# The mixer of a two-layer encoder on one Trainium2 core: background jobs on a credit clock, or one written order

## The chip, the cores and the metric

The kernel runs on one core of a Trainium2 chip. Its engines are PE (TensorE, matmuls and transposes), DVE (VectorE), ACT (ScalarE), POOL (GpSimd) and SP (SyncE, which here only issues DMAs). Each engine runs its own instructions strictly in program order, so an instruction that waits holds back everything behind it on that engine. The metric is the device time of one execution in microseconds (us), as the median of runs. Beside it stands the span of the profiled execution, from its first to its last instruction, to which all times of rows refer.

## What is computed

One sequence of 512 rows and 1024 columns goes through two layers. Only the first half of the first layer, the conv and state-space mixer, is touched by the change:

```python
def conv_ssm_layer(h, w_in, ...):              # h = rms_norm(x, mix_norm)
    z = h @ w_in                               # 1024 -> 512 (za) + 512 (zg) + 512 (u)
    ya = conformer_conv(za, zg, ...)           # za*sigmoid(zg), 31 taps, layer norm, silu
    yb = s5_mixer(u, ...)                      # scan forwards and backwards, 64 complex states a group
    return concatenate([ya, yb]) @ w_out
def s5_direction(u, ...):                      # once on u, once on u flipped in time
    bu = einsum('bsgc,gnc->bsgn', u, b)        # 32 groups of 16 channels
    s = associative_scan(a, coef * bu)
    return einsum('bsgn,gcn->bsgc', s, c)
```

After it come a gated feed-forward layer, a neighbourhood attention and a second feed-forward layer, whose code is the same before and after.

## The kernel before

The input projection `z` is three groups of fp32 matmuls: 4 weight chunks of 512 KB for `u`, 4 for the gate `zg` and 4 for `za`. A chunk is used by 8 products of 128x512 outputs (the trace counts each fp32 product as two matmul rows). The `u` group is issued at once. The 64 products of `zg` and `za` are handed out one by one by `heavy(n)`, which issues the next n of them on PE, so that PE has work between the small steps of the state-space part.

The state-space part cuts the sequence into 64 chunks of 8 rows and the 32 groups into 8 pieces of 4 groups. For every piece i there are:

- `make_pb(i)`: DVE builds the B products (six operations of 128x512) in a buffer;
- `piece_t(i)`: PE transposes them (P), ACT copies the two results (`ppb`) and fills `CB`;
- the K matmuls, whose result ACT copies to `kf`;
- the v matmuls (`U` is the transposed `u`), whose result ACT copies to `vt`;
- `g_turn(i)`: DVE multiplies phase tables, ACT copies one third of them with its sign changed;
- `g_scan(i)`: ACT fills the decays `dk` (tile rstdB), DVE turns v by the phases, runs two scans, turns the result back and writes the states S.

In the code of before, these DVE jobs are Python generators in a list (`bgV`). `tick(ns)` gives the list credit in nominal nanoseconds, and the jobs' DVE instructions are issued as the credit lasts; `finish(job)` issues the rest of a job where its result is needed. The loop issues `piece_t(i)`, then `heavy(2)`, then for the piece before it K, `heavy(1)`, v, and at the end `heavy(3)`. The backward half of v is turned round by a second ACT copy with a negative step. The B products have three buffers of their own.

The weights come through `Weights`. The first 12 chunks are used as they are, through all nine weight buffers (tags wraw, whi, wlo, three each). All later chunks are split into a high part (ACT, `whi`) and a low part (DVE, `wlo`), up to two chunks ahead of their use.

Behind the pieces, `to_chunks(an, ...)` transposes the gated input of the convolution (64 small PE transposes, 8 ACT copies). 112 ACT operations then build the banded tap matrices, PE convolves in 16 steps, and DVE evacuates 4 times and takes row sums. In the same stretch DVE builds Q (48 operations), the output matrices of the scan, again on credit: `tick(1350)` at each convolution step. `out_y` uses Q on PE; `ln_mean` and `ln_scale` are the layer norm; then the two branches are transposed (cT, yT), and `out_half` starts the output projection (`wo`).

Of the kernel before, what the change touches and what calls it, by code (L numbers as in the profile page):

```python
# [9 lines left out]
F32 = mybir.dt.float32  # L10
# [3 lines left out]
ALU = mybir.AluOpType  # L14
# [7 lines left out]
HP = (2, 1, 3)  # L22
XT = 600
UT = 5200
MT = 6000
H1 = 4
# [4 lines left out]
ZT, ME, ZC = 500, -4000, -1000  # L31
# [25 lines left out]
class Weights:  # L57
# [4 lines left out]
    def __init__(self, nc, pool, aps, whole=0):  # L62

        self.nc, self.pool, self.aps, self.whole = nc, pool, aps, whole
        self.raw, self.hl = {}, {}
        self.n_raw = self.n_hl = self.pos = 0
        self.on_pool, self.charge = (), None

    def load(self):
        i = self.n_raw  # L70
        if i >= len(self.aps):
            return
        ap = self.aps[i]
        a, b = ap.shape[1], ap.shape[2]
        tag = "wraw"
        if i < self.whole:
            tag = ("wraw", "whi", "wlo")[i % 3]
        t = self.pool.tile([P, a, b], F32, tag=tag, name=tag, bufs=self.RAW)
        self.nc.sync.dma_start(out=t, in_=ap)
        self.raw[i] = t  # L80
        self.n_raw += 1
# [40 lines left out]
def tile_hybrid_encoder(ctx, tc, x, mix_norm, ffn_norm, ffn_w_gate, ffn_w_up, ffn_w_down,  # L122
# [219 lines left out]
    def big4(shape):  # L342
        return ep.tile(shape, F32, tag="big4", name="big4", bufs=3)
# [22 lines left out]
    A.activation(out=un[:, 0, 0], in_=ones[:, 0:16], func=AF.Silu)  # L366
# [29 lines left out]
    W.load()  # L396
# [7 lines left out]
    W.load()  # L404
# [106 lines left out]
    def g_params():  # L511
# [61 lines left out]
        make_pb(0)  # L573
        job_phase.append(bgV.add(g_phase()))
        make_pb(1)
        make_pb(2)

# [9 lines left out]
    NPC, job_phase = 8, []  # L587
    PB, PBS, job_pb = {}, [P, 4, 8, 16], []
# [7 lines left out]
    def make_pb(i):  # L596
        PB[i] = big4([P, 2, 4, 8, 16])
        job_pb.append(bgV.add(g_pb(i)))
# [16 lines left out]
    job_par = bgV.add(g_params())  # L615
    tick(3000)
    xT, pxs = [], []
    xg = xp.tile([P, KD, S], F32, tag="xgh", name="xg")
    for k in range(KD):
        ps = (psa if k < 4 else psb)("xT")  # L620
        for j in range(4):
            PE.transpose(out=ps[:, j * P:(j + 1) * P], in_=xn[j][:, k * P:(k + 1) * P], identity=ident)
        pxs.append(ps)
        if k == 0:
            ps = psb("vec0")
            PE.transpose(out=ps[:, 0:16], in_=vecs[0:16], identity=ident[0:16, 0:16])
            V.tensor_copy(out=col[:, 0:16], in_=ps[:, 0:16])
        t = xtile("xT")
        A.activation(out=t, in_=pxs[k], func=AF.Copy)
        A.activation(out=xg[:, k], in_=pxs[k], func=AF.Copy, scale=col[:, R_MIX0 + k:R_MIX0 + k + 1])  # L630
        xT.append(t)
        tick(XT)
    W.ahead()
# [3 lines left out]
    for i in range(4):  # L637
# [16 lines left out]
        tick(UT)  # L654
        if i == 1:
            ps = psb("vec")
# [16 lines left out]
            V.tensor_tensor(out=gqk, in0=col[:, R_QK:R_QK + 1], in1=col[:, R_QK + 1:R_QK + 2], op=ALU.mult)  # L673
        if i == 2:
            for r in range(2):
                ps = psb("ct")
                for t in range(4):
                    PE.transpose(out=ps[:, t * P:(t + 1) * P],
                                 in_=cnat[r][:, t].rearrange("p d n -> p (d n)"), identity=ident)
                A.activation(out=CT[:, r], in_=ps.rearrange("p (g c) -> p g c", c=16), func=AF.Copy,  # L680
                             scale=-1.0 if r else 1.0)
    for j in range(4):
        A.activation(out=un[:, :, j], in_=pu[j].rearrange("p (g c) -> p g c", c=16),
                     func=AF.Copy, scale=rs0[:, j:j + 1])
# [40 lines left out]
    heavy(H1)  # L725
# [16 lines left out]
    to_chunks(un, U)  # L742

# [7 lines left out]
    vin, phase, job_scan = {}, {}, []  # L751
# [43 lines left out]
    ppb = ep.tile([P, 2, 2, 4, P], F32, tag="un", name="ppb")  # L795

    def piece_t(i):
        bgV.finish(job_pb[i])
        for q in range(2):
# [4 lines left out]
            A.activation(out=ppb[:, i % 2, q], in_=ps.rearrange("p (g n) -> p g n", g=4), func=AF.Copy)  # L804
# [5 lines left out]
    def piece_m(i):  # L810
        g0 = 4 * i
        pb, cb, pp = PB.pop(i), CB[i % 2], ppb[:, i % 2]
        def part_k():
            pk = psb("K")
            for g in range(4):
                for q in range(2):
                    w = pb[:, q, g].rearrange("p b c -> p (b c)")
                    for c in range(0, P, KW):
                        PE.matmul(out=pk[c:c + KW, g * 32:g * 32 + 32], lhsT=w[:, c:c + KW],
                                  rhs=cb[:, q, g].rearrange("p d c -> p (d c)"),  # L820
                                  start=(q == 0), stop=(q == 1))
            A.activation(out=kf[:, :, g0:g0 + 4],
                         in_=pk[:, 0:128].rearrange("p (g d c) -> p d g c", g=4, d=2), func=AF.Copy)

        part_k()
        heavy(HP[1])
# [11 lines left out]
        job_scan.append(bgV.add(g_scan(i)))  # L838

    bgV.finish(job_par)  # L840
    bgV.finish(job_phase[0])
    for v, q, r, sg in ((0, 0, 0, 1.0), (0, 1, 1, 1.0), (1, 0, 1, -1.0), (1, 1, 0, 1.0)):
        A.activation(out=low[v][:, :, :, q], in_=et[:, r, :, 0].rearrange("p e g -> p g e"), func=AF.Copy,
                 scale=sg)
    for i in range(NPC + 1):
        if i < NPC:
            piece_t(i)
            heavy(HP[0])
        if i > 0:
            if i > 2:  # L850
                bgV.finish(job_scan[i - 3])
            bgV.add(g_turn(i - 1))
            piece_m(i - 1)
            if i + 2 < NPC:
                make_pb(i + 2)
            if i == NPC:
                for h in range(2):
                    PL.tensor_tensor(out=pair[:, 64 * h:64 * h + 64], in0=ident[:, 0:64], in1=ident[:, 64:128], op=ALU.add)
                PL.tensor_scalar(out=pair, in0=pair, scalar1=1.0 / 512, scalar2=1.0, op0=ALU.mult, op1=ALU.mult)
                dm = pbp([P, G, 16])  # L860
                PL.tensor_tensor(out=dm, in0=dcol.unsqueeze(2).to_broadcast([P, G, 16]),
                                 in1=dmask.unsqueeze(1).to_broadcast([P, G, 16]), op=ALU.mult)
            tick(MT if i < NPC else ME)
            heavy(HP[2])
# [19 lines left out]

    heavy(100)
    V.tensor_reduce(out=mask16, in_=ident.rearrange("p (b c) -> p c b", c=16), axis=AX.X, op=ALU.add)
    for j in job_scan:
        bgV.finish(j)
# [60 lines left out]
    for b in range(4):  # L949
        ps = psa("conv")  # L950
        for gi in range(4):
# [10 lines left out]
            tick(1350)  # L962
# [551 lines left out]
```

## Time and profile before

| | |
|---|---|
| median of 3 runs | 1292.23 us (1291.77 to 1293.13) |
| the profiled execution | 1291.65 us |
| its span | 1289.7 us |
| PE busy | 1225.2 us, 95% of the span |
| DVE busy | 675.1 us, 52% |
| ACT busy | 471.4 us, 37% |
| POOL busy | 38.1 us, 3% |

The busy shares are averages over stages with different limits. The mixer takes the first 305 us or so; in it the engines take turns in ending the waits, while later PE is busy almost without a break. In the rows, "idle before" is the time the engine stood still ahead of an instruction, with what ended it.

### The profile page before, as it was taken

The numbers are of one execution on the slowest core, as the hardware profiler recorded it, in microseconds if no ns is written. First come the engines' busy times: TensorE is split into PE (matmuls) and PEld (weight loads), VectorE is DVE, ScalarE is ACT, GpSimd is POOL, SyncE is SP. The second block draws the span as 40 slices with busy tenths as digits, with TensorE's granted clock in tenths as the row PEclk, the third lists the DMA queues.
The fourth block names the chain that finished last, engine by engine and source line by source line (L and its number), as shares of the span: only waits on it lengthen the run. The fifth ranks groups of instructions, "written<-read, shape, count | busy, mean of one in ns | idle before, by whom it ended". The sixth has DMA issues, their size and how long they took to land.

```text
span 1289.7 us, 16189 instructions
## 1 busy us (share of the span) xinstructions
PE 1225.2 (95%) x6427; PEld 966.2 (75%) x6427; DVE 675.1 (52%) x1166; ACT 471.4 (37%) x830; POOL 38.1 (3%) x90
## 2 busy tenths in 40 slices
PE   4988867899999999999999999999999999999998
PEld 2544457788888888888888888667888888888886
DVE  4778875866444444433335563664544444443321
ACT  4335277554322333222233544653332223332110
POOL 1000000000000000000000000430000000000000
PEclk9998889899999999999999999999999999999999
DMA  8600140033333333333344542222333333332241
GB/s 158 179 2 1 49 104 2 17 99 100 97 98 99 98 97 94 95 91 95 101 141 127 153 142 72 83 75 71 93 99 98 98 98 98 98 98 82 95 134 33
DMA packets 173155, 118.04 MB, mean 92 GB/s; under 512 B 21193, under 2 KB 153593, under 8 KB 173080
## 3 DMA queue, kind: packets, MB, share of 16 engines
q1 hardware_dynamic: 172616, 115.92, 31.5%
q10 hardware_dynamic: 400, 1.07, 0.4%
q8 instruction: 50, 0.82, 0.3%
q14 instruction: 25, 0.20, 0.1%
q0 software_dynamic: 64, 0.03, 0.0%
HBM read 109.04 MB, written 7.96 MB: 91 GB/s over the span
## 4 chain that ended last, share of the span: by engine, by line
PE 82%; ACT 3%; DVE 1%; issue 0%; POOL 0%; ACTq 0%; DVEq 0%; POOLq 0%
PE gate L208 6%; PE up L208 6%; PE gate L207 6%; PE up L207 6%; PE up L206 6%; PE gate L206 6%; PE qkv L1379 3%; PE qkv L1381 3%; PE qkv L1380 3%; PE dn L208 3%; PE dn L207 3%; PE dn L206 3%; PE dn L1480 3%; PE dn L1478 3%; PE dn L1479 3%; PE o L1341 2%
## 5 line engine op out<-in xcount | busy, mean ns | idle before, releaser
L98 DVE TENSOR_TENSOR wlo<-wraw,whi 128x1024 fp32r<-128x1024 f32 x176 | 212.9, 1213 | 256.8 <-ACT whi L96 255.5
L96 ACT ACTIVATE whi<-wraw 128x1024 fp32r<-128x1024 f32 x176 | 183.4, 1044 | 283.5 <-issue 113.9
L206 PE MATMUL gate<-xgh,whi 128*128 128x512 f32 x352 | 137.2, 390 | 0.0
L206 PE MATMUL up<-xgh,whi 128*128 128x512 f32 x352 | 137.1, 390 | 0.0
L208 PE MATMUL gate<-xgh,wlo 128*128 128x512 f32 x352 | 137.0, 389 | 0.0
L208 PE MATMUL up<-xgh,wlo 128*128 128x512 f32 x352 | 137.0, 389 | 0.0
L207 PE MATMUL gate<-xgl,whi 128*128 128x512 f32 x352 | 136.9, 389 | 0.0
L207 PE MATMUL up<-xgl,whi 128*128 128x512 f32 x352 | 136.9, 389 | 0.0
L1163 DVE TENSOR_TENSOR fu<-up,rstdB 128x512 f32<-128x512 f32 x44 | 30.4, 691 | 113.4 <-PE up L208 113.4
L1165 ACT ACTIVATE gh<-fu 128x512 fp32r<-128x512 f32 x44 | 27.8, 632 | 150.8 <-DVE fu L1164 150.8
L207 PEld LDWEIGHTS gate<-xgl,whi 128*128 128x128 f32 x352 | 66.1, 188 | 13.9
L206 PEld LDWEIGHTS up<-xgh,whi 128*128 128x128 f32 x352 | 66.2, 188 | 13.8
L207 PEld LDWEIGHTS up<-xgl,whi 128*128 128x128 f32 x352 | 66.0, 188 | 13.7
L206 PEld LDWEIGHTS gate<-xgh,whi 128*128 128x128 f32 x352 | 66.0, 187 | 13.7
L208 PEld LDWEIGHTS gate<-xgh,wlo 128*128 128x128 f32 x352 | 66.1, 188 | 13.5
L208 PEld LDWEIGHTS up<-xgh,wlo 128*128 128x128 f32 x352 | 66.0, 188 | 13.6
L206 PE MATMUL dn<-gh,whi 128*128 128x512 f32 x176 | 69.3, 394 | 0.0
L207 PE MATMUL dn<-gl,whi 128*128 128x512 f32 x176 | 69.3, 394 | 0.0
L208 PE MATMUL dn<-gh,wlo 128*128 128x512 f32 x176 | 69.3, 394 | 0.0
L1480 PE MATMUL dn<-whi,gl 128*128 128x512 f32 x176 | 69.2, 393 | 0.0
L1478 PE MATMUL dn<-whi,gh 128*128 128x512 f32 x176 | 69.0, 392 | 0.0
L1379 PE MATMUL qkv<-whi,xgh 128*128 128x512 f32 x176 | 68.8, 391 | 0.0
(306 smaller groups left out, 2077.2 us busy)
## 6 DMA issues: line engine op xcount, KB each, us to landing
wraw<-in_ffn_w_gate_dram SPq DMA_DIRECT2D x44, 512.0 KB
wraw<-in_ffn_w_up_dram SPq DMA_DIRECT2D x44, 512.0 KB
wraw<-in_ffn_w_down_dram SPq DMA_DIRECT2D x38, 512.0 KB
wraw<-in_na_w_qkv_dram SPq DMA_DIRECT2D x24, 512.0 KB
bt<-bd SPq DMA_DIRECT2D x8, 640.0 KB
wraw<-in_ab_w_out_dram SPq DMA_DIRECT2D x8, 512.0 KB
wraw<-in_na_w_out_dram SPq DMA_DIRECT2D x8, 512.0 KB
wraw<-in_ffn_w_down_dram SPq DMA_DIRECT2D x8, 384.0 KB
```

The lines of the kernel that those rows point to most:

```text
L96: self.nc.scalar.activation(out=hi, in_=raw, func=AF.Copy)
L98: eng.tensor_tensor(out=lo, in0=raw, in1=hi.bitcast(F32), op=ALU.subtract)
L206: PE.matmul(out=o, lhsT=lh, rhs=rh, start=start, stop=False)
L207: PE.matmul(out=o, lhsT=lh, rhs=rl, start=False, stop=False)
L208: PE.matmul(out=o, lhsT=ll, rhs=rh, start=False, stop=stop)
L1163: V.tensor_tensor(out=u, in0=pu, in1=rB, op=ALU.mult)
L1379: PE.matmul(out=pq[j], lhsT=lh, rhs=wh[:, kk], start=(k == 0), stop=False)
L1380: PE.matmul(out=pq[j], lhsT=lh, rhs=wl[:, kk], start=False, stop=False)
L1381: PE.matmul(out=pq[j], lhsT=ll, rhs=wh[:, kk], start=False, stop=(k == 7))
L1478: PE.matmul(out=pd[j], lhsT=gh[:, k, c], rhs=wh[:, kk], start=(k == 0), stop=False)
L1479: PE.matmul(out=pd[j], lhsT=gh[:, k, c], rhs=wl[:, kk], start=False, stop=False)
L1480: PE.matmul(out=pd[j], lhsT=gl[:, k, c], rhs=wh[:, kk], start=False, stop=(k == NF - 1))
```

## The change

The mixer's background jobs are taken out of the credit list and written in one fixed order. In parts:

- Start: `mix_norm` goes ahead of x in SP's queue, x ahead of ACT's table load, and three weight chunks follow x ahead of the B parameters. The parameter chain on DVE runs through without a copy of `col` in it (ACT makes that copy). x is transposed tile by tile instead of column by column.
- Buffers: the unsplit chunks use only the three wraw buffers; the B products go into the six whi and wlo buffers. `hold` keeps the loading three chunks ahead and allows no split before the pieces are done.
- Pieces: `piece_t(0)`, K(0), `piece_t(1)`, K(1) run before `u` is transposed; then in the loop v(i), `heavy(3)`, P and K of piece i+2, `heavy(4)`, and on DVE scan(i), turn(i+2), B products of i+4.
- v: the backward half reads `U` in reverse in the matmul, so one ACT copy is left.
- `tick(2200)` instead of `tick(1350)` at each convolution step.

```diff
     def ahead(self):
-        if self.pos < self.whole:
-            while self.n_raw < min(self.pos + 8, self.whole + 1):
+        if self.hold:
+            while self.n_raw < self.pos + self.RAW:
                 self.load()
             return
...
-    def big4(shape):
-        return ep.tile(shape, F32, tag="big4", name="big4", bufs=3)
+    def big4(shape, i):
+        tag = ("whi", "wlo")[i % 2]
+        return wp.tile(shape, F32, tag=tag, name="pb", bufs=3)
...
+    load_vec(nc.sync, R_MIX0, mix_norm)
     for j in range(4):
         load_x(j)
-    load_vec(nc.sync, R_MIX0, mix_norm)
-    W.load()
+    A.activation(out=un[:, 0, 0], in_=ones[:, 0:16], func=AF.Silu)
+    for _ in range(3):
+        W.load()
...
+    ps = psb("vec0")
+    PE.transpose(out=ps[:, 0:16], in_=vecs[0:16], identity=ident[0:16, 0:16])
+    A.activation(out=col[:, 0:16], in_=ps[:, 0:16], func=AF.Copy)
+    for g in (g_params(),):
+        for _ in g:
+            pass
+    make_pb(0)
...
-                              rhs=U[:, g0 + g], start=True, stop=True)
+                              rhs=U[:, g0 + g] if c == 0 else U[:, g0 + g, ::-1], start=True, stop=True)
         v = ep.tile([P, 2, 256], F32, tag="vt", name="vt", bufs=2)
-        A.activation(out=v[0:64], in_=pv[0:64].rearrange("p (q n) -> p q n", q=2), func=AF.Copy)
-        A.activation(out=v[64:128].rearrange("p q (g k) -> p (q g) k", g=4)[:, :, ::-1],
-                     in_=pv[64:128].rearrange("p (a k) -> p a k", k=NCH), func=AF.Copy)
+        A.activation(out=v, in_=pv.rearrange("p (q n) -> p q n", q=2), func=AF.Copy)
...
+    pieces_tk(0, 1)
+    to_chunks(un, U)
+    run(g_turn(0))
+    make_pb(3)
+    run(g_turn(1))
+    for i in range(NPC):
+        piece_v(i)
+        heavy(HV[0])
+        if i + 2 < NPC:
+            pieces_tk(i + 2)
+        heavy(HV[1])
+        run(g_scan(i))
+        if i + 2 < NPC:
+            run(g_turn(i + 2))
+        if i + 4 < NPC:
+            make_pb(i + 4)
...
     heavy(100)
+    W.hold = False
...
-            tick(1350)
+            tick(2200)
```

ACT inside the piece loop, one round, of before (vt is the copy of v, rstdB the decays of the scan, ppb and CB the copies behind the transposes, kf the copy of K):

```order
L767 ACTIVATE phase_112<-phase_112 128x256
L834 ACTIVATE vt<-v 64x512
L835 ACTIVATE vt<-v 64x8x64
L774 ACTIVATE rstdB<-mag 128x4x63
L804 ACTIVATE ppb<-P 128x512 x2
L808 ACTIVATE CB_149<-CT 64x8x16 x2
```

The same engine and place in the change, from v(3) on:

```order
L830 ACTIVATE vt<-v 128x512
L799 ACTIVATE ppb<-P 128x512 x2
L803 ACTIVATE CB_150<-CT 64x8x16 x2
L816 ACTIVATE kf<-K 128x2x64
L699 ACTIVATE an<-zg,hrs 128x32x16
L700 ACTIVATE an<-an,hrs 128x32x16
L699 ACTIVATE an<-zg,hrs 128x32x16
L700 ACTIVATE an<-an,hrs 128x32x16
L770 ACTIVATE rstdB<-mag 128x4x63
L763 ACTIVATE phase_117<-phase_117 128x256
```

The decays of scan(i) stood right behind vt(i); now the copies of piece i+2, its kf and (in this round) two gate pairs `an` stand between them, and the phase copy of turn(i+2) stands ahead of the next vt.

DVE from the last convolution evacuation to the layer norm's root, of before (an<-conv is the evacuation, lns the row sums, sq and Q the building of Q, rs_a the first of twelve small operations of the root; the pair sq and Q stands there seven times, and is shown once):

```order
L964 TENSOR_TENSOR an<-conv,rstdB 128x8x64
L966 TENSOR_REDUCE lns<-an 128x8
L1034 TENSOR_TENSOR an<-an,mean 128x1024 x2
L443 TENSOR_TENSOR sq<-pwQ,CT 128x512 x2
L443 TENSOR_TENSOR Q<-sq 128x512
...
L225 TENSOR_SCALAR rs_a<-var 128x8
```

The same place in the change, from the last of the Q rows on:

```order
L436 TENSOR_TENSOR sq<-pwQ,CT 128x512 x2
L436 TENSOR_TENSOR Q<-sq 128x512
L960 TENSOR_TENSOR an<-conv,rstdB 128x8x64
L962 TENSOR_REDUCE lns<-an 128x8
L1030 TENSOR_TENSOR an<-an,mean 128x1024 x2
L218 TENSOR_SCALAR rs_a<-var 128x8
```

All 48 Q operations now stand ahead of the last evacuation; before, 21 of them stood between the mean and the root.

ACT around the first split weights, of before: the splits of the first two `w_out` chunks stand at the end of the pieces, ahead of the copies of the convolution's input AC.

```order
L868 ACTIVATE pwQ<-pw 64x256
L774 ACTIVATE rstdB<-mag 128x4x63
L96 ACTIVATE whi<-wraw 128x1024 x2
L739 ACTIVATE AC<-U 64x8x64 x8
```

In the change they stand behind the first half of the gelu (sq, tanh into sqacc, ygs), together with the split of the chunk after them:

```order
L999 ACTIVATE AC<-yT 128x512 x4
L1005 ACTIVATE sq<-AC 128x512 x2
L1009 ACTIVATE sqacc<-sqacc 128x512 x2
L1013 ACTIVATE ygs<-AC 128x512 x2
L89 ACTIVATE whi<-wraw 128x1024 x3
L1005 ACTIVATE sq<-AC 128x512 x2
```

On PE nothing stands between the transposes yT and the first `wo` product, which reads `whi` of the first of these chunks.

## Rows read from the trace of the kernel before

**Rows 1.** Windows: stretch, length, busy PE PEld DVE ACT POOL, PE clock, DMA, GB/s.

```profile
92.00:164.40 72.40, 58.76 (x432) 30.77 (x432) 60.48 (x78) 26.12 (x58) 2.34 (x2) 0.88 0.09 23
171.74:220.20 48.46, 36.58 (x433) 34.34 (x433) 27.52 (x42) 40.56 (x120) 0.25 (x2) 0.92 0.22 51
220.20:241.88 21.68, 15.44 (x156) 13.52 (x155) 19.48 (x40) 6.04 (x22) 0.00 (x0) 0.76 0.00 1
262.00:1289.70 1027.70, 1021.91 (x4826) 830.42 (x4824) 483.35 (x787) 342.55 (x529) 29.03 (x66) 1.00 0.33 98
```

**Rows 2.** Timeline of ACT's queue and PE at the start: start us, us.

```profile
9.87 1.12 ACTq L376 DMA_DIRECT2D an<-in_x_dram  x2
18.54 0.47 PE L622 MATMUL xT<-ident,an 128*128 128x128 f32 x1 [1.50 <-DMA an<-in_x_dram]
24.00 7.03 PE L649 MATMUL u<-wraw,xg 128*128 128x512 f32 x16
```

**Rows 3.** Timeline of DVE: the parameters at the start, and the third B product.

```profile
8.26 0.18 DVE L450 TENSOR_SCALAR work<-par 128x32 f32<-128x32 f32 x1
...
19.27 0.17 DVE L627 COPY col<-vec 128x16 f32<-128x16 f32 x1 [6.64 <-PE vec L626]
...
57.75 0.69 DVE L443 TENSOR_TENSOR big<-work 128x512 f32<-128x512 f32 x1
```

**Rows 4.** Timeline of DVE through one round of the piece loop.

```profile
98.98 1.23 DVE L443 TENSOR_TENSOR work<-phase,vt 128x1024 f32<-128x1024 f32 x1 [1.63 <-ACT vt L835]
...
101.04 1.27 DVE L785 TENSOR_TENSOR_SCAN sqacc<-rstdB,vt 128x256 f32<-128x256 f32 x2
...
105.01 0.69 DVE L443 TENSOR_TENSOR work<-pwP,bbar 128x512 f32<-128x512 f32 x1
...
109.19 1.29 DVE L443 TENSOR_TENSOR work<-et,sq 128x512 f32<-128x512 f32 x2
...
113.13 1.23 DVE L443 TENSOR_TENSOR work<-phase,vt 128x1024 f32<-128x1024 f32 x1 [1.57 <-ACT vt L835]
```

**Rows 5.** Timeline of PE inside the piece loop.

```profile
69.23 2.84 PE L700 MATMUL zg<-wlo,xg 128*128 128x512 f32 x6
71.91 1.04 PE L802 MATMUL P<-ident,big 128*128 128x128 f32 x8
...
98.71 1.12 PE L819 MATMUL K<-CB,big 128*64 128x32 f32 x32
...
110.18 3.62 PE L700 MATMUL zg<-whi,xg 128*128 128x512 f32 x4
```

**Rows 6.** Timeline of ACT: copies of U, of P, CB, and a phase copy.

```profile
57.29 4.89 ACT L739 ACTIVATE U<-U 64x512 f32<-64x512 f32 x8 [3.31 <-PE U L736]
...
64.36 1.06 ACT L804 ACTIVATE ppb<-P 128x512 f32<-128x512 f32 x2
65.32 0.62 ACT L808 ACTIVATE CB<-CT 64x128 f32<-64x128 f32 x2
...
111.60 0.42 ACT L767 ACTIVATE phase<-phase 128x256 f32<-128x256 f32 x1 [8.87 <-DVE phase L443]
```

**Rows 7.** Timeline from the pieces to the convolution: PE, ACT.

```profile
171.74 5.21 PE L736 MATMUL U<-ident,an 64*64 64x64 f32 x64 [7.34 <-DVE an L709]
...
173.38 4.92 ACT L739 ACTIVATE AC<-U 64x512 f32<-64x512 f32 x8 [7.01 <-PE U L736]
```

**Rows 8.** Timeline of the layer norm: ACT, DVE.

```profile
225.65 0.19 ACT L1038 ACTIVATION_READ_ACCUMULATOR diag<-an 128x1 f32 x1
...
237.81 0.16 DVE L225 TENSOR_SCALAR rs_a<-var 128x8 f32<-128x8 f32 x1
```

**Rows 9.** Timeline at the output projection: PE, ACT, DVE.

```profile
245.04 0.50 PE L206 MATMUL wo<-mah,whi 128*128 128x512 f32 x1
...
251.89 1.04 ACT L96 ACTIVATE whi<-wraw 128x1024 fp32r<-128x1024 f32 x1
...
252.97 1.22 DVE L98 TENSOR_TENSOR wlo<-wraw,whi 128x1024 fp32r<-128x1024 f32 x1 [0.26 <-ACT whi L96]
```

More of the change, by code (lines that the diff above doesn't have):

```diff
@@ L62, in __init__ @@
     def __init__(self, nc, pool, aps, whole=0):
-        self.nc, self.pool, self.aps, self.whole = nc, pool, aps, whole
+        self.nc, self.pool, self.aps, self.whole, self.hold = nc, pool, aps, whole, whole > 0
         self.raw, self.hl = {}, {}
@@ L74, in load @@
         a, b = ap.shape[1], ap.shape[2]
[L75 to L78, printed above, removed]
+        t = self.pool.tile([P, a, b], F32, tag="wraw", name="wraw", bufs=self.RAW)
         self.nc.sync.dma_start(out=t, in_=ap)
@@ L596, in make_pb @@
     def make_pb(i):
-        PB[i] = big4([P, 2, 4, 8, 16])
-        job_pb.append(bgV.add(g_pb(i)))
+        PB[i] = big4([P, 2, 4, 8, 16], i)
+        for _ in g_pb(i):
+            pass
     def g_pb(i):
@@ L614, in tile_hybrid_encoder @@
     V.tensor_copy(out=par, in_=pp0[:, 0:96].rearrange("p (a g) -> p a g", a=3))
-    job_par = bgV.add(g_params())
-    tick(3000)
-    xT, pxs = [], []
+    ps = psb("vec0")
[3 more added lines that the diff above has]
+        for _ in g:
+            pass
+    make_pb(0)
+    xT = []
     xg = xp.tile([P, KD, S], F32, tag="xgh", name="xg")
+    pxs = [(psa if k < 4 else psb)("xT") for k in range(KD)]
+    for j in range(4):
+        for k in range(KD):
+            PE.transpose(out=pxs[k][:, j * P:(j + 1) * P], in_=xn[j][:, k * P:(k + 1) * P], identity=ident)
     for k in range(KD):
[L620 to L627, printed above, removed]
         t = xtile("xT")
+        A.activation(out=xg[:, k], in_=pxs[k], func=AF.Copy, scale=col[:, R_MIX0 + k:R_MIX0 + k + 1])
         A.activation(out=t, in_=pxs[k], func=AF.Copy)
-        A.activation(out=xg[:, k], in_=pxs[k], func=AF.Copy, scale=col[:, R_MIX0 + k:R_MIX0 + k + 1])
         xT.append(t)
-        tick(XT)
-    W.ahead()
     pu = [psa("u") for _ in range(4)]
@@ L653, in tile_hybrid_encoder @@
             V.tensor_scalar(out=hrs, in0=rs0, scalar1=0.5, scalar2=None, op0=ALU.mult)
-        tick(UT)
         if i == 1:
+            for _ in g_phase():
+                pass
+            make_pb(1)
+            make_pb(2)
             ps = psb("vec")
@@ L681, in tile_hybrid_encoder @@
                              scale=-1.0 if r else 1.0)
+            for v, q, r, sg in ((0, 0, 0, 1.0), (0, 1, 1, 1.0), (1, 0, 1, -1.0), (1, 1, 0, 1.0)):
+                A.activation(out=low[v][:, :, :, q], in_=et[:, r, :, 0].rearrange("p e g -> p g e"), func=AF.Copy,
+                             scale=sg)
     for j in range(4):
@@ L750, in tile_hybrid_encoder, with run @@
     PL.memset(decays[:, :, :, 0:1], 0.0)
-    vin, phase, job_scan = {}, {}, []
+    vin, phase = {}, {}
+    def run(*gens):
+        for g in gens:
+            for _ in g:
+                pass
     def g_turn(i):
@@ L794, in tile_hybrid_encoder @@
     kf = pt([P, 2, G, 16], "kf", ep)
[L795 removed]
+    ppb = xp.tile([P, 4, 2, 4, P], F32, tag="xgl", name="ppb")
     def piece_t(i):
[L798 removed]
         for q in range(2):
@@ L808, in piece_t, with piece_k, piece_v @@
             A.activation(out=cb[h, :, :, d], in_=CT[h, :, 4 * i:4 * i + 4], func=AF.Copy)
-    def piece_m(i):
+    def piece_k(i):
         g0 = 4 * i
[L812 to L826, printed above, removed]
+        pb, cb = PB.pop(i), CB[i % 2]
+        pk = psb("K")
+        for g in range(4):
+            for q in range(2):
+                w = pb[:, q, g].rearrange("p b c -> p (b c)")
+                for c in range(0, P, KW):
+                    PE.matmul(out=pk[c:c + KW, g * 32:g * 32 + 32], lhsT=w[:, c:c + KW],
+                              rhs=cb[:, q, g].rearrange("p d c -> p (d c)"),
+                              start=(q == 0), stop=(q == 1))
+        A.activation(out=kf[:, :, g0:g0 + 4],
+                     in_=pk[:, 0:128].rearrange("p (g d c) -> p d g c", g=4, d=2), func=AF.Copy)
+    def piece_v(i):
+        g0 = 4 * i
+        pp = ppb[:, i % 4]
         pv = psb("v")
@@ L837, in piece_m @@
         vin[i] = v
[L838 to L846, printed above, removed]
-            piece_t(i)
[L848 to L864, printed above, removed]
@@ new lines, in pieces_tk @@
+    def pieces_tk(*ii):
+        for i in ii:
+            piece_t(i)
+            piece_k(i)
+    pieces_tk(0, 1)
[14 more added lines that the diff above has]
+            make_pb(i + 4)
+        if i == 1:
+            V.tensor_tensor(out=gqk, in0=col[:, R_QK:R_QK + 1], in1=col[:, R_QK + 1:R_QK + 2], op=ALU.mult)
@@ L865, in tile_hybrid_encoder @@
+    for h in range(2):
+        PL.tensor_tensor(out=pair[:, 64 * h:64 * h + 64], in0=ident[:, 0:64], in1=ident[:, 64:128], op=ALU.add)
+    PL.tensor_scalar(out=pair, in0=pair, scalar1=1.0 / 512, scalar2=1.0, op0=ALU.mult, op1=ALU.mult)
+    dm = pbp([P, G, 16])
+    PL.tensor_tensor(out=dm, in0=dcol.unsqueeze(2).to_broadcast([P, G, 16]),
+                     in1=dmask.unsqueeze(1).to_broadcast([P, G, 16]), op=ALU.mult)
     f, b = slice(0, 64), slice(64, 128)
@@ L883, in tile_hybrid_encoder @@
     PL.dma_start(out=kd_ap(7, 1), in_=kfr[0:16, 1], accum_op=ALU.add)
+    V.tensor_reduce(out=mask16, in_=ident.rearrange("p (b c) -> p c b", c=16), axis=AX.X, op=ALU.add)
     heavy(100)
-    V.tensor_reduce(out=mask16, in_=ident.rearrange("p (b c) -> p c b", c=16), axis=AX.X, op=ALU.add)
-    for j in job_scan:
-        bgV.finish(j)
+    W.hold = False
     early.close()
```

24 lines of the change are left out of this document (5 added, 19 removed).

## The prediction

> **What bounds the kernel now.** I read the windows first, to see which stages have room. From 262.00 to the end PE is busy 1021.91 of 1027.70 us [rows 1]; the code there is the same, so that stretch only shifts, and all that the change can give or cost lies ahead of 262. There the bound changes hands. From 92 to 164.4 DVE is busy 60.48 of 72.40 us and PE's clock is 0.88 of full: DVE ends most waits. From 171.74 to 220.20 it is ACT (40.56 of 48.46). From 220.20 to 241.88 DVE again (19.48 of 21.68) [rows 1]. Then I read the timelines at the borders. The `u` products begin at 24.00, 5.46 us after the last x tile landed at 18.54 [rows 2]. In the pieces DVE's period is 14.15 us, from 98.98 to 113.13, 1.57 of it idle for vt [rows 4]. PE had done its projections long before the convolution's input, and stood 7.34 us for DVE until 171.74 [rows 7]. And the layer norm's root began at 237.81 although its last input, on ACT, was ready at 225.84 [rows 8]: DVE was building Q.
>
> The profiled execution took 1291.65 us, span 1289.7, so 1.95 lie around the span; it is 0.58 under the median. I sum three terms against it, in the order of the program.
>
> **Term A, the start of the convolution.** *x.* ACT's last two x issues ended at 10.99 and the last landed at 18.54, 7.5 us later, among weights and B parameters [rows 2]. In the change they wait only for lam and the first x half, so I put their issue near 7; the flight lies between some 3 us (no rivals) and 7.5 (the row). I take 5.5, last x at 12.5, range 10 to 15. Then, as before, 8 ACT copies free the banks; that took 5.46 [rows 2], and with most transposes done already I take 4.8: `u` begins at 17.3. Four chunks at 7.03 [rows 2] and 1.0 of small transposes are 29.1; PE will have stood before it, 1.5 for a low clock. `u` ends at 47.9.
>
> *From u to the first scan.* P(0) runs beside the last `un` copy, which ends 0.9 after `u`; then come P's copies (1.06) and CB (0.62) [rows 6], and K(0) at 50.6, P(1) at 51.7, K(1) at 54.1, since each K follows its P at once and must wait for these copies, about 2.4 from P's start. `U` starts at 55.1 and goes at the pace of its eight copies, 4.89 [rows 6]: 60.6. v(0) takes what K takes, 1.12 [rows 5]; with its copy, scan(0) starts at 62.5. DVE is not what it waits for: its early work ran from 8.26 to 58.44, with 6.64 of a wait for `col` that goes [rows 3], so 43.5; with a start near 5 and turn(0), turn(1), B(3) added (9 us, below) it ends near 58.
>
> *The loop.* From the rows of one round [rows 4]: scan 6.03 (98.98 to 105.01), its scan instructions, which read the decays, 2.06 after its start; B 4.18; turn 2.4. On PE a product is 0.9 (six matmul rows from 69.23, next at 71.91), P 0.9 to the next, K 1.1 [rows 5]. DVE alone would go through 8 scans, 6 turns and 4 B in 79.4, to 142. But the orders say that the engines hold one another. The decays of scan(i) now stand on ACT behind kf of piece i+2, so behind v(i), three products (2.7), P with its copies (2.4), K (1.1) and two short ACT operations (0.7): 6.9 after v(i). The copies for K(i+2) stand on ACT behind vt(i), and that behind the phase copy of turn(i+1), for which ACT waits as it did 8.87 us [rows 6]. So PE can't run ahead of DVE, nor DVE ahead of PE. Walking it: scan(0) starts at 62.5 and is held 4.1 for its decays (68.7); turn and B follow, scan(1) 79.3, scan(2) 91.9, scan(3) 104.4. In rounds 3 and 4 the gate pairs stand ahead of the decays too: held 3.8 and 3.6. scan(4) starts at 120.9, scan(5), now with no B ahead of it to cover the phase copy and vt, at 134. K(7) stands at 135.7. Behind it PE has K, 26 products, v(6) and v(7), 1.1 + 23.4 + 2.2, and 1 for a low clock after its stand: 163.4; the last `an` product 0.65, so the convolution's transposes begin at 164.0 on PE's time, DVE having ended near 157. PE comes warm there; the first copy to AC follows after 0.9 instead of 1.64: 164.9 against 173.38 [rows 7]. **A = -8.5.** Bounds: with no holding PE's 8 rounds of 10.8 and 8 products end near 155, -17.7; with 79 us of PE work at the granted 0.88 [rows 1] 10.7 more than unslowed, +2.
>
> The reversed read of `U` on PE has no row; I take the forward cost, below it nothing, above it as much again, 0.6 a piece; the copy that goes was 0.6 on ACT. Both lie beside DVE's round. The three weight buffers: a chunk is asked for when PE leaves the buffer, two chunks (14 products, 12.6 us) ahead of its use; nothing. The kd writes now stand on SP behind the load that waits for the eleventh chunk; they end about 2 us before AC needs their memory, so they are hidden by PE's last 8 products; without that cover it would be 2 to 4.
>
> **The convolution** is ACT's tap building, 48.46 us [rows 1], unchanged. DVE was busy 27.52 of these [rows 1], and the 21 Q operations that move in here, 0.69 each as any of this size [rows 4], add 14.4: 42 of 48, hidden, barely.
>
> **Term B, the layer norm.** With no Q behind the mean, the root waits for ACT's last sum, 225.84, and the small matmul behind it, some 0.6: 226.5 in place of 237.81 [rows 8]. What follows is as before. **B = -11.3**, bounds -12 and -9 if the last evacuation comes late.
>
> **Term C, the first split weight.** Before, the first two `w_out` chunks were split at the pieces' end, on ACT and DVE with nothing late for it, and `wo` began at 245.04 [rows 9]. Now they stand behind the first gelu half. Before, one split stood just there: whi at 251.89 to 252.93, wlo 252.97 to 254.19 [rows 9]. In the change the first chunk takes that place, `wo`'s third matmul needs wlo, and PE, with nothing else to do, stands from 245.50 to 254.19 in before's frame: 8.7. Then its clock is low: after short stands in the pieces four matmul rows took 3.62 instead of 1.8 [rows 5], so 0 to 3, I take 2. The second gelu half comes 2 later but glu is 8.7 later itself. **C = +10.7**, bounds 8.7 and 12.
>
> Sum: -8.5 - 11.3 + 10.7 = -9.1, 1291.65 to 1282.5, and 1283.1 in the median's terms; I say **1282.6**.
>
> **The rivals.** *Each burst cold (slower).* The change puts a stand in every round on PE, between P and K. If PE falls to 1.2 of its 2.4 GHz after each, a product costs 1.8 instead of 0.9, as in [rows 5]; I count about 4 in the loop so already. From 13 or 14 more of the 64 on (12 us) the time is no shorter; with 16 it is 1295. For it: 0.88 and 0.76 granted in [rows 1]. Against it: DVE's rounds are longer than PE's, so part is hidden. The Trainium skill, page "TensorE: Matmul & The Clock Gate", section "HAM oscillation — how this bites in real kernels", says that idle gaps between bursts bring the clock down and each burst then starts cold; by that rule this rival's sum would stand. The trace agrees with the fall, not that every gap brings it: [rows 1] would show 0.5 then, not 0.88.
>
> *No holding.* If ACT's order costs nothing, A is -17.7: 1291.65 - 18.3 = 1273.4. For it: DVE's and PE's rounds are close, and stands may overlap. Against it: the decays' place.
>
> *x doesn't come earlier*, because the same transfers share the same engines: last x at 18.5, all of A's walk 6 later, A = -2.5: 1288.5. Against it: the B parameters now queue behind x.
>
> *Q stays half in the way*, DVE being late at the evacuations: B = -5.6, 1288.3.
>
> **How the numbers follow.** Chances: the forecast 0.52 (1277.5 to 1287 by its own bounds), no holding 0.20, cold bursts 0.10, x no earlier 0.08, Q 0.04, the rest 0.06, spread on both sides. Range 1272 to 1290: it takes in no holding, late x and late Q, and leaves out most of the cold case and the outer rest. A measurement of this kernel tells about 0.2%, 2.6 us, from no change: faster is below 1289.6. Faster 0.83, the same 0.08, slower 0.09.
>
> **What the profile after would show.** `u` from about 17; scan(0) from 62.5 with its scan instructions held near 4 us for ACT; DVE's rounds without the 1.57 wait while B products last; PE standing between P and K; the convolution's transposes near 164; no Q behind the mean, the root some 5 us after the mean; and a stand of some 9 us on PE ahead of the first `wo`, ended by ACT whi and DVE wlo. Wrong would be: the transposes ahead of 158 or behind 170, no stand at `wo`, or a different length of the stretch behind it.

## The result, and the profile after

The changed kernel takes 1276.93 us (median of 4 runs, 1276.18 to 1277.73) against 1292.38 us of the kernel before, run beside it on the same chip (4 runs, 1291.77 to 1293.13): a ratio of 0.988 with a 95% interval of 0.9863 to 0.9897, 15.5 us less. The profiled execution took 1276.18 us with a span of 1274.5, against 1291.65 and 1289.7: 15.2 us of span.

All of it lies ahead of the feed-forward layers. Windows of the kernel after, cut where its stages begin (columns as in [rows 1]):

```profile
77.35:149.78 72.43, 58.46 (x437) 32.28 (x436) 59.18 (x76) 21.75 (x49) 1.26 (x1) 0.88 0.12 37
159.36:206.18 46.82, 33.13 (x418) 30.58 (x413) 39.15 (x59) 40.57 (x120) 0.00 (x0) 1.00 0.26 59
206.18:216.38 10.20, 9.90 (x155) 9.61 (x154) 5.76 (x19) 6.04 (x22) 0.00 (x0) 1.00 0.01 2
246.80:1274.50 1027.70, 1022.19 (x4827) 830.62 (x4825) 483.04 (x787) 342.63 (x528) 29.02 (x66) 1.00 0.33 98
```

The last 1027.70 us, cut to the same length as in [rows 1], hold the same work: PE is busy 1022.19 us against 1021.91, and the counts of operations agree to within one. In the convolution ACT is as busy as before (40.57 against 40.56) and sets the stage, while DVE has risen to 39.15 from 25.99 (the kernel before from its first AC copy on, 173.38 to 220.20): that is Q, whose rows take 31.91 us here and took 17.93 there. The layer norm's window, which held 19.48 us of DVE before, holds 5.76.

Timeline of PE at the start of the kernel after (answers [rows 2]):

```profile
8.26 3.78 PE L617 MATMUL xT<-ident,U 128*128 128x128 f32 x16 [2.56 <-DMA U<-in_x_dram]
11.83 3.24 PE L617 MATMUL xT<-ident,an 128*128 128x128 f32 x16
15.63 14.62 PE L638 MATMUL u<-wraw,xg 128*128 128x512 f32 x32 [0.56 <-ACT xT L621]
```

PE transposes each tile as it lands, and `u` begins at 15.63 instead of 24.00, after a stand of 0.56 us.

Timelines of DVE and PE in the piece loop, after (answers [rows 4, 5, 7]): the scans that wait for their decays, v(0), and the K matmuls that wait for the copies of P, two of them with the products behind them (one at half clock, one at full).

```profile
64.67 1.27 DVE L781 TENSOR_TENSOR_SCAN sqacc<-rstdB,vt 128x256 f32<-128x256 f32 x2 [3.01 <-ACT rstdB L770]
106.69 1.27 DVE L781 TENSOR_TENSOR_SCAN sqacc<-rstdB,vt 128x256 f32<-128x256 f32 x2 [4.13 <-ACT rstdB L770]
122.76 1.27 DVE L781 TENSOR_TENSOR_SCAN sqacc<-rstdB,vt 128x256 f32<-128x256 f32 x2 [3.49 <-ACT rstdB L770]
...
56.66 1.15 PE L827 MATMUL v<-U,ppb 128*64 128x64 f32 x32
...
86.24 1.92 PE L813 MATMUL K<-CB,pb 128*64 128x32 f32 x32 [3.19 <-ACT CB L803]
88.09 5.96 PE L694 MATMUL zg<-wraw,xg 128*128 128x512 f32 x8
...
116.92 1.92 PE L813 MATMUL K<-CB,pb 128*64 128x32 f32 x32 [7.41 <-ACT CB L803]
131.59 1.12 PE L813 MATMUL K<-CB,pb 128*64 128x32 f32 x32 [2.11 <-ACT CB L803]
132.64 3.70 PE L694 MATMUL za<-wraw,xg 128*128 128x512 f32 x8
...
158.57 3.93 PE L729 MATMUL U<-ident,an 64*64 64x64 f32 x64 [0.78 <-DVE an L703]
```

DVE stands 3 to 4 us at a time in front of a scan whose input is there, for a fill of 0.40 us that stands too far back in ACT's order; PE stands up to 7.41 us ahead of K. Still the convolution's transposes begin at 158.57 instead of 171.74.

Timelines of DVE, ACT and PE from the layer norm to the output projection, after (answers [rows 8, 9]):

```profile
207.27 2.35 DVE L1030 TENSOR_TENSOR an<-an,mean 128x1024 f32<-128x1024 f32 x2 [2.20 <-PE mean L1026]
212.31 0.17 DVE L218 TENSOR_SCALAR rs_a<-var 128x8 f32<-128x8 f32 x1 [2.69 <-PE var L1039]
...
226.56 2.94 ACT L89 ACTIVATE whi<-wraw 128x1024 fp32r<-128x1024 f32 x3
...
227.63 3.50 DVE L91 TENSOR_TENSOR wlo<-wraw,whi 128x1024 fp32r<-128x1024 f32 x3 [0.26 <-ACT whi L89]
...
227.65 0.80 PE L199 MATMUL wo<-mah,whi 128*128 128x512 f32 x1 [7.87 <-ACT whi L89]
```

No Q stands behind the mean any more, and the root follows it by 5.04 us (212.31 instead of 237.81). And PE, which had nothing else, stands 7.87 us for the first split weight.

### The profile page after: what moved, and what is told of

Same layout as the page of the kernel before. It is cut to its first block, busy times and chain, and to the rows that moved or that the text cites. A ratio compares the mean times of both kernels' runs of the same rounds, so it can differ in the third digit from the quotient of the medians.

```text
span 1274.5 us, 16175 instructions
## 1 busy us (share of the span) xinstructions
PE 1218.3 (96%) x6427; PEld 962.4 (76%) x6427; DVE 676.6 (53%) x1165; ACT 466.6 (37%) x823; POOL 36.7 (3%) x90
## 4 chain that ended last, share of the span: by engine, by line
PE 89%; ACT 5%; DVE 3%; DMA 1%; SPq 1%; issue 1%; POOL 0%; DVEq 0%; ACTq 0%; POOLq 0%
PE up L199 6%; PE gate L199 6%; PE gate L200 6%; PE up L200 6%; PE gate L201 6%; PE up L201 6%; PE qkv L1375 3%; PE qkv L1377 3%; PE qkv L1376 3%; PE dn L199 3%; PE dn L201 3%; PE dn L200 3%; PE dn L1476 3%; PE dn L1474 3%; PE dn L1475 3%; PE o L1337 3%
```

## The experiments

Eleven kernels ran, each beside the kernel before; differences are of medians, against 1276.93 us of the changed kernel unless another is named, and stages are compared by the profiled executions. The kernel before had a median of 1292.38 to 1292.71 us in every session, so medians of different sessions can be compared. The 95% interval of a ratio is some 1.8 us to either side; a smaller difference is not clear of noise.

### Term A: ACT's order

**The decays right behind vt.** The fill is taken out of `g_scan` and issued in `piece_v`:

```diff
@@ piece_v(i)
         vin[i] = v
+        A.activation(out=decays[:, i % 2, :, 1:], in_=m8[:, 1, 4 * i:4 * i + 4]..., func=AF.Copy)
@@ g_scan(i)
-        A.activation(out=dk[:, :, 1:], in_=m8[:, 1, gs]..., func=AF.Copy)
```

> The changed kernel with ACT's fill of the decays moved from behind the copies for K(i+2) to right behind the copy of v(i). The holds of DVE's scans for the decays (3.01, 4.13, 3.49 and 1.46 us) should go. Theory: ACT's order holds DVE, and DVE's phase copies hold ACT and through it PE, so PE's stands ahead of K shrink with the holds: the convolution's transposes come 5 to 10 us earlier, 1267 to 1272 us. Rival: PE's own sequence (64 products, 8 rounds of P, K and v, with a stand for the copies in each) sets the end of the loop; DVE only stands elsewhere then, and the time falls by less than 2 us, 1275 to 1277 us.

Measured: 1268.92 us, ratio 0.9815 (0.9801 to 0.9828), -8.0 us. No scan waits for a decay. Timeline of PE with the decays early:

```profile
96.14 1.92 PE L812 MATMUL K<-CB,pb 128*64 128x32 f32 x32 [2.68 <-ACT CB L802]
...
121.47 1.13 PE L812 MATMUL K<-CB,pb 128*64 128x32 f32 x32 [1.76 <-ACT CB L802]
...
150.14 3.93 PE L729 MATMUL U<-ident,an 64*64 64x64 f32 x64 [0.78 <-DVE an L703]
```

The longest stand ahead of K falls from 7.41 to 2.68 us, the stands there sum to 9.6 us in place of 16.6, and the transposes come 8.43 us earlier. So DVE, ACT and PE did hold one another: a 0.4 us fill held the scan, the scan held the next phase table, its copy on ACT held the copies of P, and those PE.

**The start order undone.**

```diff
-    load_vec(nc.sync, R_MIX0, mix_norm)
     for j in range(4):
         load_x(j)
-    A.activation(out=un[:, 0, 0], in_=ones[:, 0:16], func=AF.Silu)
-    for _ in range(3):
-        W.load()
+    load_vec(nc.sync, R_MIX0, mix_norm)
+    W.load()
```

Silu stands ahead of the x issues again, and the other two W.load() behind the B parameters and behind the convolution's weights.

> The changed kernel with the queue order at the start undone: mix_norm behind x, the table load of ACT ahead of x, one weight chunk behind x, the others behind the B parameters as in the kernel before. Theory: u starts later by about the 8.4 us by which the change moved it (15.63 against 24.00), v(0) follows PE and ACT all the way, and the loop keeps the shift: +5 to +8 us, 1282 to 1285 us. Rival: DVE's own early work (it ends at 57.77, and the first scan waited only 1.94 us behind it) sets the first scan, and the order of x is worth less than 2 us, 1277 to 1279 us.

Measured: 1282.81 us, ratio 0.9921 (0.9907 to 0.9936), +5.9 us. Timelines of PE and DVE of that kernel:

```profile
18.93 1.10 PE L618 MATMUL xT<-ident,an 128*128 128x128 f32 x8 [0.44 <-DMA an<-in_x_dram]
20.59 3.90 PE L639 MATMUL u<-wraw,xg 128*128 128x512 f32 x7 [0.57 <-ACT xT L622]
...
64.36 1.22 DVE L437 TENSOR_TENSOR work<-phase,vt 128x1024 f32<-128x1024 f32 x1 [6.05 <-ACT vt L831]
```

The last x tile lands at 18.9, as before ([rows 2]: 18.54), and all the shift of `u` (4.96 us) reaches the first scan (4.66): DVE stood 6.05 us for vt. x comes earlier by its queues, and nothing hides it. (The profiled execution is 6.9 us longer than that of the changed kernel; most of the rest is a longer hold: scan(3) waited 6.06 us for its decays instead of 4.13.) But `u` begins at 20.59, not at 24.00: the other 3.4 us of its 8.4 are not the queues'.

**x transposed by columns.**

```diff
-    for j in range(4):
-        for k in range(KD):
+    for k in range(KD):
+        for j in range(4):
             PE.transpose(out=pxs[k][:, j * P:(j + 1) * P], ...)
```

> The changed kernel with x transposed column by column again (all four tiles of a column, then the next column), the queues and all else as changed. In the kernel before, u started 5.46 us after the last x tile had landed; in the changed kernel it started 1.8 us or so after it, since most transposes were done and PE warm. Theory: the order of the transposes is what made that difference; u starts 2 to 4 us later and the loop keeps it: 1279 to 1281 us. Rival (the prediction's own count): ACT's copies set it, which take a column at a time either way, and only PE's lower clock costs something; 0 to +1.5 us, 1277 to 1278.5 us.

Measured: 1279.53 us, ratio 0.990 (0.9883 to 0.9916), +2.6 us. Timeline of PE of that kernel:

```profile
13.60 0.48 PE L617 MATMUL xT<-ident,an 128*128 128x128 f32 x1 [1.96 <-DMA an<-in_x_dram]
...
17.71 0.61 PE L617 MATMUL xT<-ident,an 128*128 128x128 f32 x2
18.14 0.40 PE L617 MATMUL xT<-ident,U 128*128 128x128 f32 x2
...
19.03 7.46 PE L638 MATMUL u<-wraw,xg 128*128 128x512 f32 x17
```

With the last tile at 13.60, 28 transposes are still to do, 0.21 us each until 18.14 and 0.11 after it, and `u` begins without a wait 5.43 us after that tile, as in [rows 2]. This is the missing 3.4 us: what filled the time before `u` was PE's slow transposes, not ACT's copies. Their pace has the ratio of PE's two clock levels, but the profile gives a granted clock of 1.00 for both stretches, so that the clock made them slow is not shown.

**Two copies of v.** The rows read by PE are forward again, and ACT reverses:

```diff
-                              rhs=U[:, g0 + g] if c == 0 else U[:, g0 + g, ::-1], ...
+                              rhs=U[:, g0 + g], ...
-        A.activation(out=v, in_=pv..., func=AF.Copy)
+        A.activation(out=v[0:64], in_=pv[0:64]..., func=AF.Copy)
+        A.activation(out=v[64:128]...[:, :, ::-1], in_=pv[64:128]..., func=AF.Copy)
```

> The changed kernel with the reversal of v undone: U is read forwards in both halves, and ACT turns the backward half round in a second copy. Theory: the reversed read costs PE nothing and the copy that went was hidden on ACT, except where ACT's order holds DVE's scans for the decays behind vt (some four rounds, 0.6 us each at most); 0 to +2 us, 1277 to 1279 us. Rival: the reversed read slows PE (above its 1.12 us for 32 matmul rows) and the time falls by 1 to 5 us, 1272 to 1276 us.

Measured: 1280.37 us (1278.63 to 1281.96), ratio 0.9908 (0.9894 to 0.9922), +3.4 us; the profiled execution, the fastest of these, +2.4. Timeline of PE of that kernel:

```profile
56.39 1.15 PE L827 MATMUL v<-U,ppb 128*64 128x64 f32 x32
...
132.39 1.54 PE L813 MATMUL K<-CB,pb 128*64 128x32 f32 x32 [3.24 <-ACT CB L803]
133.86 4.90 PE L694 MATMUL za<-wraw,xg 128*128 128x512 f32 x8
```

The rival falls: 32 matmul rows of v take 1.15 us in both. The theory has the place right and the size too small. DVE waits for vt, the copy that is now two, 1.56 us instead of 0.97 in two rounds; its waits for the decays hardly grow in sum (12.33 us against 12.09). PE's longest stand ahead of K grew from 7.41 to 8.15, and the next one from 2.11 to 3.24. Behind that one PE's clock was low (granted 0.67 over K, then 0.50): K took 1.54 us instead of 1.12 and the eight rows behind it 4.90 instead of 3.70, 1.6 us that the theory had not counted.

### Term B: the credit of the convolution's steps

**Back to 1350.**

```diff
-            tick(2200)
+            tick(1350)
```

> The changed kernel with the credit of the convolution's steps put back from 2200 to 1350. Theory (term B): Q again stands between the mean and the root on DVE, and the time grows by what was gained there, +11.5 us, 1288.4 us. Rival: with the splits late, PE stands 7.87 us at wo anyway and part of a later layer norm falls into that stand; then +3 to +7, 1280 to 1284 us.

Measured: 1287.0 us, ratio 0.9955 (0.9942 to 0.9967), +10.1 us. Timeline of DVE with the credit at 1350:

```profile
208.44 2.35 DVE L1030 TENSOR_TENSOR an<-an,mean 128x1024 f32<-128x1024 f32 x2 [2.20 <-PE mean L1026]
210.70 1.29 DVE L436 TENSOR_TENSOR sq<-pwQ,CT 128x512 f32<-128x512 f32 x2
...
222.91 0.16 DVE L218 TENSOR_SCALAR rs_a<-var 128x8 f32<-128x8 f32 x1
```

Six pieces of Q (sq twice and Q once) stand between mean and root again, and from the one to the other it takes 14.47 us instead of 5.04, 9.4 more. (The root comes 10.6 us later in all; the other 1.2 lie ahead of the mean, where this edit changes nothing.) The rival, that the stand at `wo` takes up part of it, falls: PE stands 7.87 us there, as in the changed kernel. The 9.4 us are one piece of Q, 2.05 us, below the theory's 11.5: six were left over here, seven in the kernel before.

**The kernel before with 2200 alone.** The same line in the other kernel.

> The kernel before with nothing but the credit of the convolution's steps raised from 1350 to 2200. Theory (term B stands alone): the Q operations that stood between the mean and the root move into the convolution, which ACT sets; -11.5 us, 1280.9 us. Rival: in the kernel before DVE comes late into the convolution and still owes scans and the tap builds, so the 21 moved operations (14.4 us) make its evacuations late and half comes back: -3 to -7 us, 1285 to 1289 us.

Measured: 1280.94 us, ratio 0.991 (0.9897 to 0.9924), 11.7 us below the kernel before in the same session (1292.66). The mean's subtraction begins at 222.95 and the root at 228.00, 5.05 us behind it; in the kernel before they were 16.53 us apart (221.28 and 237.81). Term B stands alone: it needs no other part of the change.

### Term C: the first split weights

**Split at the end of the pieces again.**

```diff
     make_tc(1, 1)
+    W.ahead()
```

> The changed kernel with one thing undone: the first two w_out chunks are again split at the end of the pieces, behind the two DVE tap builds. Theory (term C): the 7.87 us stand on PE ahead of the first wo, with the half clock behind it and the second gelu half held behind three splits, goes; the first tanh of glu stood 29.49 us behind the layer norm's scaling and should stand near 19.0 again, as in the kernel before. That gives -10.3 us, 1266.6 us. Rival: the two wlo operations (1.2 us each) and the whi operations push DVE and ACT late in the convolution, where DVE's slack is small, and 2.4 us or more come back, 1269 us or later. Second rival: the stand is not the path, since the second gelu half ends last anyway; then less than 3 us are gained, 1274 us or later.

Measured: 1266.44 us, ratio 0.9801 (0.9788 to 0.9815), -10.5 us. Timelines of PE and ACT of that kernel:

```profile
219.84 0.50 PE L199 MATMUL wo<-mah,whi 128*128 128x512 f32 x1
...
154.93 1.06 ACT L89 ACTIVATE whi<-wraw 128x1024 fp32r<-128x1024 f32 x1 [6.64 <-DMA wraw<-in_ab_w_out_dram]
...
234.07 0.67 ACT L1116 ACTIVATE sq<-glu,hgb_gqk 128x512 f32<-128x512 f32 x1
```

`wo` begins 7.81 us earlier with no wait, and the first tanh of glu (sq<-glu) at 234.07 in place of 244.21. The splits found room where ACT stood idle: it waited 6.64 us there for the second chunk. The 2.35 us of wlo that DVE got ahead of Q moved nothing: the root came at 212.42 in place of 212.31.

### What is next on the path

**Splits and decays early together** (both edits above).

> The changed kernel with both the split of the first two w_out chunks at the end of the pieces and the decays filled right behind vt. Theory: the two gains lie in different stages and add, -10.5 and -8.0: 1258.4 us. Rival: ACT and DVE share the stretch at the end of the pieces, and the splits, which wait for a weight chunk there, come late for the convolution; 2 to 4 us of the sum are missing, 1260.5 to 1262.5 us.

Measured: 1257.40 us, ratio 0.9728 (0.9715 to 0.9742), -19.5 us; the two alone sum to -18.5. They lie in different stages and add, within the noise.

**Two products between P and K**, on top of these:

```diff
-HV = (3, 4)
+HV = (2, 4)
             piece_t(i)
+            if i > 1:
+                heavy(2)
             piece_k(i)
```

> As the kernel with the splits and the decays early, but with two products between P and K of every piece of the loop (two, P, two, K, four in place of three, P, K, four), so that the copies of P run beside products. Theory: PE's stands ahead of K (1.26 to 2.68 us in six rounds, 9.6 in all with the decays early) end the loop later, and most go: 4 to 6 us less than with the two alone, near 1253.5 us. Rival: DVE's rounds of 12.4 us set the loop by then, DVE ended its last scan's work only 7 us ahead of PE, and v of the next piece comes later behind the added products; less than 2 us, 1257 us or more.

Measured: 1256.53 us, ratio 0.9722 (0.9708 to 0.9736), -0.9 us against the kernel with the two alone, which is not clear of noise (1256.06 to 1257.50 against 1257.01 to 1258.05): the rival's size, but not for its whole reason. Timelines of PE, ACT and SP:

```profile
147.99 2.36 PE L729 MATMUL U<-ident,an 64*64 64x64 f32 x32 [4.84 <-DVE an L703]
...
150.75 4.92 ACT L732 ACTIVATE AC<-U 64x512 f32<-64x512 f32 x8 [9.87 <-DMA kd<-kf]
...
143.18 0.37 SPq L72 DMA_DIRECT2D wraw<-in_ssm_glu_w_dram  x1
143.60 1.15 SPq L879 DMA_DIRECT2D kd<-kf  x2
```

PE's loop did get shorter (its last product ended 4.84 us ahead of the transposes), and two other walls stood behind it: DVE's last `an`, and the kd writes, which stand on SP behind loads of weights and were not done when AC needed their memory.

**The kd writes behind the last K.** They and the POOL work ahead of them are issued in the loop, ahead of the last two weight loads:

```diff
+        if i == 5:
+            kd_out()        # pair, dm, kf += dm, the five kd writes, from behind the loop
```

> As the kernel with two products between P and K, but with the kd writes and the POOL work ahead of them issued behind K of the last piece, so ahead of the last two loads of weights on SP. There the first AC copy waited for the kd writes until 150.75 while PE's transposes had stood ready from 147.99. Theory: the writes were the next wall, and the AC copies come right behind PE's transposes, some 0.8 us after them: -1.9 us, 1254.6 us. Rival: the splits and the AC copies are held by DVE's last an products and tap builds as much, and nothing is gained, 1256 to 1257 us.

Measured: 1255.12 us, ratio 0.9711 (0.9696 to 0.9725), -1.4 us against the one before, between theory and rival; the runs do not overlap (1255.71 at most against 1256.06 at least), but the intervals do. The first AC copy comes at 148.03 instead of 150.75 and now waits for PE's transposes, which wait 4.84 us for `an`.

**The last scan ahead of the last an products.**

```diff
         piece_v(i)
+        if i == 7:
+            run(g_scan(i))      # and not below
         heavy(HV[0])
```

> As the kernel with the kd writes early, and the last scan issued on DVE ahead of the last products of an, its mask behind them. In the kernel with two products between P and K, DVE waited 1.34 and 1.03 us for za products ahead of that scan, and PE stood 4.84 us for an behind it. Theory: DVE does the scan in the time in which it waited, an is ready 2.5 us earlier, and the convolution with it: 2 to 2.6 us below the kernel with the kd writes early. Rival: ACT's second split, which waits for its weight chunk until PE has left chunk ten, ends last then; less than 1 us.

Measured: 1251.81 us, ratio 0.9685 (0.967 to 0.9699), -3.3 us against the one before, 25.1 under the changed kernel. That is somewhat more than the theory's 2 to 2.6; the transposes begin 2.55 us earlier (144.26 against 146.81). Timeline of DVE:

```profile
135.70 1.23 DVE L436 TENSOR_TENSOR work<-phase,vt 128x1024 f32<-128x1024 f32 x1
...
141.73 2.48 DVE L703 TENSOR_TENSOR an<-an,za 128x512 f32<-128x512 f32 x4
```

The last scan runs in the time in which DVE waited for za, and all four `an` products follow without a wait. This is the fastest version found.

## Why the prediction was right, and where its sizes were off

The forecast was 1282.6 us, within 1272 to 1290. The three terms and their mechanisms hold, and the stretch behind them is of the same length. The size is another matter: 1276.93 us lies 5.7 under the forecast, just outside the bounds it gave itself (1277.5 to 1287), and 3.5 above the rival without holding (1273.4). It fell within the range because the range made room for that rival. The time alone would not decide between the two; the waits for the decays do, and the run that removed them. The convolution's transposes, at 158.57, came close to the 158 that was named as a sign of being wrong.

| term | predicted | in the profile after |
|---|---|---|
| A, first AC copy | -8.5 | -14.0 (159.36 against 173.38) |
| convolution | 0 | 0 (root -25.5 after it, A and B together) |
| B, layer norm | -11.3 | -11.5 |
| C, first split | +10.7 | +10.3 (from -25.5 to -15.2) |

**Term A was mis-sized by 5.5 us.** The lead over the forecast was 2.8 us at the first scan, 3.9 at scan(5), 4.1 at K(7) and 5.5 at the first AC copy; step by step:

- *x and `u`.* `u` was put at 17.3 and began at 15.63. It took 30.15 us where the prediction had 30.6, of which 1.5 for a low clock that did not come (its first 32 rows took 14.62 us, close to twice the 7.03 of a chunk in [rows 2]), and ended at 45.78 instead of 47.9. The step that failed is "8 ACT copies free the banks; that took 5.46": the 5.46 us were transposes at 0.21 and then 0.11 us each, as the run by columns showed, and tile by tile they ran while x was landing. x itself was later than the 12.5 put for it, if the run by columns, whose queues are the same, may stand for it (13.60). The x rival falls, since the order undone cost 5.9.
- *From `u` to v(0).* The walk let v(0) wait for all eight copies of `U`. It reads only the first groups and began at 56.66, 10.9 after the end of `u` instead of 12.7. The first scan kept 2.8 us of the lead (59.70 against 62.5), since its vt stood on ACT behind the other copies of `U`.
- *The holds.* Predicted 4.1, 3.8 and 3.6 us, measured 3.01, 4.13 and 3.49; scan(5) began at 130.10, with 3.9 us of lead. This was the part that carried the forecast away from the rival without holding, and it stands: removing the cause gave back 8.0 us. That rival's price was itself too small: with the decays early the first AC copy comes at 150.94, 22.4 us ahead of [rows 7], and not 17.7.
- *Behind K(7).* Predicted 28.3 us to the transposes with 1 for a low clock, measured 26.98. The stand of 2.11 us ahead of it left the clock alone (K 1.12 us, the eight rows behind it 3.70).

What the written order itself gave is less than term A suggests. Of the 14.0 us, 8.4 were there when `u` began; there the runs with the queue order undone (4.96) and with x by columns (3.40) account for all of it. At the first scan the lead over the kernel before was 10.9 us (59.70 against 70.58), and the whole loop behind it added 3.1, about what the second copy of v costs when it is put back (2.4 in the profiled executions). No run undid the order of the pieces, the buffers or the move of the `col` copy alone, so what each of these gave is not shown.

The forward cost of the reversed read was right: nothing. The kd writes were hidden by PE's last products, as said; the run with two products between P and K took that cover away, and there AC began 2.76 us behind PE's first transpose instead of 0.79: 2.0 us, the low end of the 2 to 4 that the prediction put on it.

**Term B** was right in place and size; Q fits into the convolution, where DVE rises to 39.15 of 46.82 us, and the rival with Q half in the way falls. **Term C** was right too. Its 8.7 us were counted to the third row of `wo`, which reads wlo; that row came at 228.91 and, with the splits early, at 220.41: 8.5 us. (The 7.87 are the stand ahead of the first row.) The price of the low clock behind it, some 1.8 of the 10.3, is in the trace: the `wo` matmul rows between 229.50 and 232.49, at a granted clock of 0.50, began every 0.43 us, the later ones every 0.23.

**Each burst cold** falls by the numbers: of six stands in the loop, two brought the half clock (those of 3.19 and 7.41 us), and the granted clock of the loop, 0.88 in the first window above, is what it was in [rows 1]. Where it came the price was as read from [rows 5]: K 1.92 us instead of 1.12, eight matmul rows 5.96 instead of the 3.70 of a full-clock group. The Trainium skill, page "TensorE: Matmul & The Clock Gate", section "HAM oscillation — how this bites in real kernels", describes a loop in which the wait ahead of every burst is long enough to bring the clock down, so that each burst starts cold. The trace agrees for two of the six stands; the prediction had put it as a rule for every gap. Two points of its case against this rival do not hold as written. A loop of cold bursts need not show 0.5 in [rows 1], since the clock came back within a burst: behind the K of 1.92 us and the 5.96 of its products, v took its full-clock 1.15. And at 0.9 us each, 10 more cold products use up the 9.1 us of the forecast, not 13 or 14; 16 more would give 1297 us, not 1295.

## What to carry to other kernels

Where engines run in a written order, follow the shortest instruction: a 0.4 us fill that stood a few rows too late held DVE, through DVE the next copy on ACT, and through that PE, 8.0 us in all. A job that waits on nothing late can be priced alone and moved into a stage that another engine sets (term B gave 11.7 us alone and 10.1 to 11.5 within the change); a job taken out of an idle stretch and put where it is first needed costs more than its own length: a split of 1.0 us on ACT and 1.2 on DVE, behind half a gelu in the order, made PE stand 7.87 us and then run on at half clock (term C). Each wall that falls shows the next, so a gain on one engine is worth only what the second wall lets through: PE's shorter loop was worth 0.9 us at most until the kd writes and the last scan were moved; the three together were worth 5.6. What the two moves would give without the shorter loop was not run.

## What the runs showed of the hardware

The length of PE's stand did not decide alone whether its clock fell. In the run with the start order undone, a stand of 3.19 us left the clock up (granted 1.00 over K and the products behind it), and one of 3.13 in the next round brought half clock (granted 0.50 over K). Timeline of PE of that run:

```profile
90.89 1.12 PE L814 MATMUL K<-CB,pb 128*64 128x32 f32 x32 [3.19 <-ACT CB L804]
91.95 3.70 PE L695 MATMUL zg<-wraw,xg 128*128 128x512 f32 x8
...
103.51 1.92 PE L814 MATMUL K<-CB,pb 128*64 128x32 f32 x32 [3.13 <-ACT CB L804]
105.36 5.99 PE L695 MATMUL zg<-wraw,xg 128*128 128x512 f32 x8
```

With the decays early a stand of 2.68 us did it (K 1.92 us). The clock could also fall only when PE was at work again, so K alone does not tell. Timeline of PE of the run with x by columns:

```profile
88.57 1.12 PE L813 MATMUL K<-CB,pb 128*64 128x32 f32 x32 [3.20 <-ACT CB L803]
89.63 5.40 PE L694 MATMUL zg<-wraw,xg 128*128 128x512 f32 x8
```

K had its full clock here, and the granted clock fell to 0.50 over the products behind it (5.40 us instead of 3.70). The same came behind a stand of only 1.76 us with the decays early (K 1.13 us, eight rows 5.40), while the stand of 2.11 us in the kernel after had no such sequel (3.70).

The same shows in the convolution: behind a stand of 3.70 us the kernel after kept its clock (40 matmul rows in 3.44 us, granted 1.00), and behind one of 3.73 us the run with early splits did not (37 in 5.78, granted 0.50). So a low clock behind a short or middling stand can be counted only as a chance. And a source of which PE read half backwards cost nothing: 1.15 us for 32 matmul rows either way.
